# A decoder layer on one core: norm roots behind whole gate blocks, gate blocks in pairs that share a bank, and small products on zeros at the start

## The chip, the cores and the metric

The kernel runs on one core of a Trainium2 chip. Times are microseconds (us) of device time for one launch. A core has five engines that run beside each other and meet through semaphores: TensorE (PE in the profile, with its weight loads as PEld), VectorE (DVE), ScalarE (ACT), GpSimd (POOL) and SyncE (SP), which only issues transfers.

## The reference

One layer of a decoder in float32, for 1024 tokens of width 1024:

```python
f1 = swiglu(rms_norm(h, ffn1_pre_g[l]), ffn1_w_in[l], ffn1_w_out[l])   # silu(gate) * up, then @ w_out; D_FF = 2816
h = h + HALF_STEP * rms_norm(f1, ffn1_post_g[l])
u = rms_norm(h, mix_pre_g[l])
p_rwkv, p_swa, q_mem, gate_logits = _split(u @ w_in[l], IN_SIZES)
...                                                    # y_a: RWKV-7, y_b: sliding window, y_c: attention into memory
mem_n = rms_norm(mem, mem_norm_g[l])                   # memory: 256 tokens; keys and values are mem_n @ w_kv
...
merged = g_a * (y_a @ w_branch[l, 0]) + g_b * (y_b @ w_branch[l, 1]) + g_c * (y_c @ w_branch[l, 2])
h = h + rms_norm(merged @ w_out[l], mix_post_g[l])
f2 = swiglu(rms_norm(h, ffn2_pre_g[l]), ffn2_w_in[l], ffn2_w_out[l])
h = h + HALF_STEP * rms_norm(f2, ffn2_post_g[l])
```

`rms_norm` divides each token by the root of its mean square, so it needs a sum over all features before any product of the normalized value can start.

## The kernel before

**Products.** Activations lie with features on the partitions and tokens on the free axis, in two halves of 512 tokens (h0, h1). Every float32 operand is split into a high part (`w_hi`, `u`) and a low part (`w_lo`, the odd tile of a pair), and each product is three matmuls in `mm3`: high by high (L247), high by low (L248), low by high (L249). Weights come from DRAM in strips of 128 x 512 (`w_raw`, 256 KB, issued by SP, four buffers); ACT makes the high part (L154), VectorE the low part (L156), and eight pairs of such operands may be alive. A strip serves 12 matmuls.

**The FFNs** use a scheme of seven products in the place of eight (Strassen and Winograd): their input is turned into factors b11, t1, t2, b22, t3, b21, t4, which are sums of quarters of the normalized x. The gate's product of one block of 128 features needs only h0: a lower half (b11, strip `lower`, 12 matmuls) and an upper half (b21, strip `upper`, 12 matmuls). Such a *gate block* of 24 matmuls can run before h1 is normalized. The first `FIRST` blocks of each FFN run so: their lower part m1 and their gate g are parked in DRAM (`first_d`) and come back later for the *rest* of the block (60 matmuls). The other blocks run whole (*pair*, 84 matmuls).

**The first FFN's start.** The first `UNSCALED` gate blocks do not wait for the norm. `unscaled_gates` multiplies x by the gain only (`split`), takes the products, and multiplies m1 and g by the reciprocal root `rs` afterwards (`finish`: m1 on POOL, L429, g on VectorE, L430). Meanwhile ACT squares x (L313) and POOL adds the squares (L317), for h0 and for h1.

**A gate block before** takes two banks of PSUM: lower in `px`, upper in `py`. ACT copies `px` away (L459), and VectorE adds it to `py` (L465); ACT then applies Silu.

**A norm's root** (`rstd`): four small matmuls with ones sum the squares over the partitions (`ps_ms`, L275); VectorE takes the reciprocal root with 13 small operations on 128 x 4 numbers (L280 to L291: `rsm`, `rsh`, `rsy`, `rsq`); four matmuls with the identity spread it over the partitions (`ps_rs`, L297). `factors_norm` then scales x by gain and root (L358), `factors_first` and `factors_part` form and split the factors (L304 and others).

**Memory.** While VectorE inverts triangular blocks for RWKV (`rwkv_invert`: L881 and L882, in a chain of steps that shrink), TensorE runs the mixer's input products. Then `memory_kv` normalizes the memory tokens by a `rstd` of its own and makes keys (`pq`, 128 x 256, scaled into `km` by VectorE) and values. The mixer's 24 gate blocks (`gate_block`, `pgate`, 48 matmuls on two strips each) follow; the first `GATES_FIRST` of them come before the RWKV chain, whose first product is `gram` (L913).

**What sets the order.** The tile framework's scheduler orders each engine's instructions; `high_priority(offset)` moves an instruction ahead by so many places (`lead` is 300, `urgent` 1000). `plan` lists the weight strips in the order in which they are loaded. PSUM has four banks for large products and four for small ones.

Of the kernel before, what the change touches and what calls it, by code (L numbers as in the profile page):

```python
# [33 lines left out]
FIRST = {"ffn1": 13, "ffn2": 13}  # L34
UNSCALED = 8
# [13 lines left out]
GATES_FIRST = 8  # L49
ATT_ROW = {f: i for i, f in enumerate(ATT_BLOCKS)}  # L50
# [32 lines left out]
class Builder:  # L83
# [4 lines left out]
    def plan(self):  # L88
        seq = []
        for f in ("ffn1", "ffn2"):  # L90
            if f == "ffn1":
                items = [(f + "_" + q, j) for q in ("lower", "upper") for j in (0, 1)]
            else:
                items = [(f + "_gate", j) for j in (0, 1)]
            items += [(f + "_gate", j) for j in range(2, FIRST[f])] + [(f + "_rest", j) for j in range(FIRST[f])]
# [16 lines left out]
        for name, i in seq:  # L112
            f, _, kind = name.partition("_")
            halves = (slice(0, 4), slice(4, 8))
            if kind in ("gate", "rest", "pair"):
                for j in (i,) if kind == "gate" else (i, i + KF):
                    self.raws += [(self.io[f + "_in"][j][:, q], "in" if j >= KF else None) for q in halves]
# [188 lines left out]
    def sum_squares(self, xs, pool, engine=None):  # L306

        nc = self.nc
        n = xs[0].shape[1]
        acc = None  # L310
        for x in xs:
            sq = pool.tile([P, n], F32, tag=f"sq{n}", name="sq", bufs=3)
            nc.scalar.activation(sq, x, ACT.Square)  # L313
            if acc is None:
                acc = sq
            else:
                (engine or nc.vector).tensor_tensor(acc, acc, sq, ALU.add)  # L317
        return acc
# [32 lines left out]
    def factors_norm(self, xs, part, gname, pool, rs=None, engine=None):  # L351
# [3 lines left out]
        if rs is None:  # L355
            rs = self.rstd([self.sum_squares(xs, pool, engine)], D, pool, hi - lo)[:, : hi - lo]
# [14 lines left out]
    def factors_begin(self, pool):  # L371
# [3 lines left out]
        self.t2, self.t3 = ([pool.tile([P, TH], F32, tag="t", name="t", bufs=8) for _ in range(KH)] for _ in (0, 1))  # L375
# [35 lines left out]
    def unscaled_gates(self, f, x, pool, first_d):  # L411

        nc, V, G = self.nc, self.nc.vector, self.nc.gpsimd
        raw = [(self.u_tile(), self.u_tile()) for _ in range(KD)]

# [7 lines left out]
        def half(name, j, xs, last):  # L423
            ps = self.psum("py" if last else "px")
            self.product(ps, self.take(f + "_" + name, j), xs, True, True)
            return ps

        def finish(m1, g):
            G.tensor_tensor(m1, m1, rs, ALU.mult)  # L429
            V.tensor_tensor(g, g, rs, ALU.mult)  # L430
            nc.scalar.activation(g, g, ACT.Silu)
            return m1, g

        split(range(KH))
        m = [self.gate_product(half("lower", j, raw[:KH], False), pool) for j in (0, 1)]
        split(range(KH, KD))
        done = [(a, self.gate_sum(half("upper", j, raw[KH:], True), a, pool)) for j, a in enumerate(m)]
        sq = self.sum_squares([t[0] for t in x], pool, G)

        def gate(j):  # L440
            a = self.gate_product(half("gate", j, raw[:KH], False), pool)
            return a, self.gate_sum(half("gate", j, raw[KH:], True), a, pool)

        done.append(gate(2))
        ps = self.rstd([sq], D, pool)
        rs = self.u_tile(F32)
        nc.scalar.copy(rs, ps)
        for j in range(UNSCALED):
            if j >= len(done):
                done.append(gate(j))  # L450
            self.store_first(first_d, j, *finish(*done[j]))
            if j == 2:
                self.factors_norm(x, HALVES[0], f + "_pre_g", pool, rs)
                self.factors_first(x)

    def gate_product(self, px, pool):
        x = pool.tile([P, TH], F32, tag="px", name="m1", bufs=3)
        with self.tc.high_priority(offset=self.urgent):
            self.nc.scalar.copy(x, px)  # L459
        return x  # L460

    def gate_sum(self, py, x, pool):
        g = pool.tile([P, TH], F32, tag="gate", name="g", bufs=5)
        with self.tc.high_priority(offset=self.urgent):
            self.nc.vector.tensor_tensor(g, py, x, ALU.add)  # L465
        return g

    def store_first(self, first_d, j, m1, g):
        self.nc.gpsimd.dma_start(first_d[j, 0], m1)
        self.nc.gpsimd.dma_start(first_d[j, 1], g)  # L470

    def ffn_in(self, f, x, fact_d, first_d, parts, norm, pre=None):

        nc, V = self.nc, self.nc.vector
        with self.tc.tile_pool(reuse_waits="tile", name="ffn_in", bufs=2) as pool:
            self.stage, self.stage_pool = "in", pool
            if pre:
# [12 lines left out]
    def ffn_in_gate(self, name, j, pool):  # L490
# [538 lines left out]
    def memory_kv(self, pool, km_d, vm_d):  # L1029
# [497 lines left out]
```

## Time and profile before

| | us |
|---|---|
| median of 3 runs (2409.64 to 2413.92) | 2411.68 |
| the profiled execution | 2412.76 |
| its span | 2411.0 |
| TensorE busy | 2310.9 |
| VectorE busy | 1674.9 |
| ScalarE busy | 975.7 |
| GpSimd busy | 266.7 |

A row of a timeline reads: start, length, engine, line, operation, output<-inputs, shapes, number, and in brackets the idle time ahead with what ended it. In a table by windows, each engine's busy time in that stretch stands with its instructions in brackets; PEclk is the granted clock of TensorE, 1.00 at full speed. Matmuls overlap, so that their spacing, not their length, is their price.

### The profile page before, as it was taken

What the parts mean: (1) busy time and instruction counts of PE and PEld (TensorE: products, weight loads), DVE (VectorE), ACT (ScalarE), POOL (GpSimd) and SP (SyncE); (2) the same over time, 40 slices, a digit from 0 to 9 for tenths busy, and PEclk for the clock granted to TensorE, in tenths of its full rate; (3) what the DMA queues carried; (4) which work ended last, traced back from release to release, by engine and by line L of the source; (5) the groups of instructions that cost most, each with busy time, mean ns of one, the idle gap of its engine ahead of it and who ended that gap; (6) DMA issues with size and microseconds to landing.
All of it is one profiled execution on the core that took longest, in us unless ns stands there. A gap on an engine that the chain in (4) does not pass through costs nothing.

```text
span 2411.0 us, 34086 instructions
## 1 busy us (share of the span) xinstructions
PE 2310.9 (96%) x12176; PEld 1872.9 (78%) x12176; DVE 1674.9 (69%) x2719; ACT 975.7 (40%) x1833; POOL 266.7 (11%) x379
## 2 busy tenths in 40 slices
PE   7799999999999999799999999999999999999997
PEld 5588888787887778678776887778887788887887
DVE  7988765676787767981444447666898786667675
ACT  6422233444545343222335445524553223344551
POOL 5311110100000000200220000042011111100000
PEclk9899999999999999999999999999999999999998
DMA  5455532587632435334334534364465543338763
GB/s 202 165 171 184 169 105 97 180 274 234 226 130 92 151 107 210 102 133 147 115 119 144 165 110 147 109 209 154 153 205 181 199 166 118 109 123 289 239 217 107
DMA packets 218441, 389.38 MB, mean 162 GB/s; under 512 B 39296, under 2 KB 67456, under 8 KB 218016
## 3 DMA queue, kind: packets, MB, share of 16 engines
q1 hardware_dynamic: 185472, 305.08, 39.2%
q0 software_dynamic: 16480, 54.01, 6.0%
q10 hardware_dynamic: 16320, 28.12, 3.4%
q8 instruction: 96, 1.57, 0.3%
q14 instruction: 73, 0.60, 0.1%
HBM read 277.55 MB, written 108.53 MB: 160 GB/s over the span
## 4 chain that ended last, share of the span: by engine, by line
PE 73%; DVE 13%; DMA 5%; issue 4%; ACT 3%; POOL 1%; SPq 0%; DVEq 0%; ACTq 0%; POOLq 0%
PE px L247 5%; PE px L248 5%; PE px L249 5%; PE pgate L247 4%; PE pgate L249 3%; PE pgate L248 3%; PE po L247 3%; PE po L248 3%; PE po L249 3%; PE pz L247 3%; PE pz L248 3%; PE pz L249 3%; PE pu L247 2%; PE pu L248 2%; PE pu L249 2%
## 5 line engine op out<-in xcount | busy, mean ns | idle before, releaser
L154 ACT CAST w_hi<-w_raw 128x512 fp32r<-128x512 f32 x566 | 349.0, 620 | 786.0 <-PE px L248 138.7
L156 DVE TENSOR_TENSOR w_lo<-w_raw,w_hi 128x512 fp32r<-128x512 f32 x558 | 401.9, 723 | 224.1 <-ACT w_hi L154 218.9
L247 PE MATMUL px<-u,w_hi 128*128 128x512 f32 x352 | 140.1, 398 | 19.7 <-ACT w_hi L154 19.1
L247 PE MATMUL po<-u,w_hi 128*128 128x512 f32 (+1 forms) x396 | 147.9, 374 | 8.1 <-DVE g L552 4.3
L247 PE MATMUL pgate<-u,w_hi 128*128 128x512 f32 x384 | 154.3, 402 | 0.0
L249 PE MATMUL pgate<-u,w_lo 128*128 128x512 f32 x384 | 153.7, 400 | 0.0
L248 PE MATMUL pgate<-u,w_hi 128*128 128x512 f32 x384 | 153.0, 398 | 0.0
L248 PE MATMUL po<-u,w_hi 128*128 128x512 f32 (+1 forms) x396 | 147.1, 372 | 0.0
L249 PE MATMUL po<-u,w_lo 128*128 128x512 f32 (+1 forms) x396 | 147.0, 371 | 0.0
L247 PE MATMUL px<-f,w_hi 128*128 128x512 f32 x352 | 137.3, 390 | 3.4 <-DVE u L518 1.6
L247 PE MATMUL pz<-u,w_hi 128*128 128x512 f32 x352 | 137.8, 391 | 2.8 <-DVE m L518 2.8
L249 PE MATMUL px<-u,w_lo 128*128 128x512 f32 x352 | 139.6, 397 | 0.2 <-DVE w_lo L156 0.2
L248 PE MATMUL px<-u,w_hi 128*128 128x512 f32 x352 | 138.9, 395 | 0.0
L249 PE MATMUL pz<-u,w_lo 128*128 128x512 f32 x352 | 137.1, 389 | 0.0
L248 PE MATMUL pz<-u,w_hi 128*128 128x512 f32 x352 | 137.0, 389 | 0.0
L248 PE MATMUL px<-f,w_hi 128*128 128x512 f32 x352 | 137.0, 389 | 0.0
L249 PE MATMUL px<-f,w_lo 128*128 128x512 f32 x352 | 137.0, 389 | 0.0
L303 ACT CAST u<-hid 128x512 fp32r<-128x512 f32 x154 | 95.1, 620 | 92.7 <-DMA hid<-fact_d 91.7
L304 DVE TENSOR_TENSOR u<-hid,u 128x512 fp32r<-128x512 f32 x154 | 105.3, 687 | 32.2 <-ACT u L303 31.4
L537 POOL DMA_DIRECT2D fact_d<-g x88 | 47.5, 539 | 606.8 <-DVE g L536 281.5
L249 PE MATMUL pu<-u,w_lo 128*128 128x512 f32 x264 | 102.7, 389 | 0.0
L248 PE MATMUL pu<-u,w_hi 128*128 128x512 f32 x264 | 102.7, 389 | 0.0
(361 smaller groups left out, 5465.7 us busy)
## 6 DMA issues: line engine op xcount, KB each, us to landing
w_raw<-in_ffn_in SPq DMA_DIRECT2D x228, 256.0 KB
w_raw<-in_ffn_out SPq DMA_DIRECT2D x198, 256.0 KB
hid<-fact_d SPq DMA_DIRECT2D x154, 256.0 KB
w_raw<-in_win SPq DMA_DIRECT2D x112, 256.0 KB
fact_d<-g POOLq DMA_DIRECT2D x88, 256.0 KB, 2.8
fact_d<-h POOLq DMA_DIRECT2D x66, 256.0 KB, 3.4
gate_d<-gate SPq DMA_DIRECT2D x24, 512.0 KB
pk_d<-pk ACTq DMA_DIRECT2D x4, 2560.0 KB
```

Of the source, the lines that this page charges most:

```text
L154: self.nc.scalar.copy(hi, x)
L156: (engine or self.nc.vector).tensor_tensor(lo, x, hi.bitcast(F32), ALU.subtract)
L247: mm(out, wh, xh, start=first, stop=False, **kw)
L248: mm(out, wh, xl, start=False, stop=False, **kw)
L249: mm(out, wl, xh, start=False, stop=last, **kw)
L303: self.nc.scalar.copy(hi, x)
L304: self.nc.vector.tensor_tensor(lo, x, hi.bitcast(F32), ALU.subtract)
L537: store = lambda n, t: nc.gpsimd.dma_start(fact_d[FACTORS.index(n), j // 2], t)
```

## The change

- *Pairs in one bank each* (`gate_pair`): two blocks j and j+1 run in the order lower j, lower j+1, upper j, upper j+1. The upper half accumulates on top of the lower half in the same bank. ACT copies the lower part out in between (the upper product must wait for that copy), and takes the Silu straight from the bank. VectorE's addition of L465 goes for the blocks that run ahead; whole blocks keep it.
- `FIRST` goes from 13 to 16 in the first FFN and from 13 to 14 in the second; `UNSCALED` from 8 to 6. Of the six, blocks 0 to 3 are scaled afterwards by VectorE, m1 and g; blocks 4 and 5 are scaled by VectorE as it takes them out of the bank (`scale`).
- POOL's sums of squares and its scalings of m1 move to VectorE.
- `rstd(between=...)`: a gate pair is emitted between the sum over the partitions and the spreading of the root, and these small matmuls keep their place in program order. In the first FFN pair (2, 3) stands there for h0 and pair (8, 9) for h1; in memory, four mixer gate blocks (`GATES_MEM`), whose strips `plan` lists ahead of memory's. `memory_norm`, the part of `memory_kv` ahead of the root, is emitted before `rwkv_invert`.
- At the start, fourteen 128 x 128 matmuls of zeros (`warm`) and one small ACT operation run while the first loads are under way; the first weight strip is issued ahead of most of x, and x is loaded from two queues.
- t3 and t2 swap the order in which their tiles are taken.

```diff
-FIRST = {"ffn1": 13, "ffn2": 13}
-UNSCALED = 8
+FIRST = {"ffn1": 16, "ffn2": 14}
+UNSCALED = 6
+WARM = 14
+GATES_MEM = 4
...
-                (engine or nc.vector).tensor_tensor(acc, acc, sq, ALU.add)
+                nc.vector.tensor_tensor(acc, acc, sq, ALU.add)
...
-        self.t2, self.t3 = ([pool.tile([P, TH], F32, tag="t", name="t", bufs=8) for _ in range(KH)] for _ in (0, 1))
+        self.t3, self.t2 = ([pool.tile([P, TH], F32, tag="t", name="t", bufs=8) for _ in range(KH)] for _ in (0, 1))
...
+        def scale(t, ps):
+            with self.tc.high_priority(offset=self.urgent):
+                V.tensor_tensor(t, ps, rs, ALU.mult)
+
+        m_tile = lambda: pool.tile([P, TH], F32, tag="t", name="m1", bufs=8)
+        self.prefetch()
+        split(range(KH))
+        done = []
+        done += self.gate_pair(f, 0, lower, upper, pool, m_tile, between=lambda: split(range(KH, KD)))
+        sq = self.sum_squares([t[0] for t in x], pool)
+        ps = self.rstd([sq], D, pool, between=lambda: done.extend(self.gate_pair(f, 2, lower, upper, pool, m_tile)))
+        rs = self.u_tile(F32)
+        with self.tc.high_priority(offset=self.lead):
+            nc.scalar.copy(rs, ps)
+        for j, (m, g) in enumerate(done):
+            V.tensor_tensor(m, m, rs, ALU.mult)
             V.tensor_tensor(g, g, rs, ALU.mult)
...
+        self.factors_norm(x, HALVES[0], f + "_pre_g", pool, rs)
+        self.factors_first(x)
+        for j in range(4, UNSCALED, 2):
+            for i, (m, g) in enumerate(self.gate_pair(f, j, lower, upper, pool, m_tile, scale)):
+                self.store_first(first_d, j + i, m, g, g)
+
+    def gate_pair(self, f, j, lower, upper, pool, m_tile, evict=None, between=None, silu=False):
+
+        def copy(t, ps, func=ACT.Copy):
+            with self.tc.high_priority(offset=self.urgent):
+                self.nc.scalar.activation(t, ps, func)
+
+        pss, ms, gs = [], [], []
+        for i in (0, 1):
+            ps = self.psum("px")
+            self.product(ps, self.take(f + "_lower", j + i), lower, True)
+            pss.append(ps)
+            ms.append(m_tile())
+            (evict or copy)(ms[-1], ps)
+        if between:
+            between()
+        for i, ps in enumerate(pss):
+            self.product(ps, self.take(f + "_upper", j + i), upper, last=True)
+            gs.append(pool.tile([P, TH], F32, tag="gate", name="g", bufs=5))
+            copy(gs[-1], ps, ACT.Silu) if silu else (evict or copy)(gs[-1], ps)
+        return list(zip(ms, gs))
...
-                self.memory_kv(mp, km_d, vm_d)
-            for g in range(GATES_FIRST):
+                self.memory_kv(mp, km_d, vm_d, lambda: [self.gate_block(g, u, gp, gate_d) for g in range(GATES_MEM)])
+            for g in range(GATES_MEM, GATES_FIRST):
                 self.gate_block(g, u, gp, gate_d)
...
+    def warm(self, x):
+        ...
+        with self.tc.high_priority(offset=self.urgent):
+            nc.vector.memset(x, 0.0)
+            nc.scalar.activation(x[:, :1], x[:, :1], ACT.Square)
+            ps = self.psum("ps_ms")
+            for _ in range(WARM):
+                nc.tensor.matmul(ps[:, :P], x[:, P : 2 * P], x[:, 2 * P : 3 * P], start=True, stop=True)
```

How the instructions stand now. First TensorE at the end of the unscaled blocks of the first FFN. Before, this was the place of the root's spreading, in the upper half of block 3 (numbers tell tiles apart; `u_126` to `u_129` are unnormalized x):

```order
L247 MATMUL py_460<-u_126,w_hi_201 128x512
L248 MATMUL py_460<-u_127,w_hi_201 128x512
L249 MATMUL py_460<-u_126,w_lo_203 128x512
L247 MATMUL py_460<-u_128,w_hi_201 128x512
L297 MATMUL ps_rs_377<-ident_68,rsy_361 128x128 x4
L248 MATMUL py_460<-u_129,w_hi_201 128x512
L249 MATMUL py_460<-u_128,w_lo_203 128x512
```

Now `ps_rs` stands 45 rows ahead of the following, which is the end of block 5 (`px_520`) and the start of pair (6, 7), the first with normalized operands `u_467` (high) and `u_468` (low):

```order
L247 MATMUL px_520<-u_144,w_hi_353 128x512
L248 MATMUL px_520<-u_145,w_hi_353 128x512
L249 MATMUL px_520<-u_144,w_lo_355 128x512
L247 MATMUL px_587<-u_467,w_hi_374 128x512
L247 MATMUL px_608<-u_467,w_hi_394 128x512
L247 MATMUL px_750<-u_467,w_hi_523 128x512
L247 MATMUL px_771<-u_467,w_hi_543 128x512
L248 MATMUL px_587<-u_468,w_hi_374 128x512
L249 MATMUL px_587<-u_467,w_lo_376 128x512
```

TensorE takes the four products of one high operand for four blocks first, and then needs its low part. VectorE at the same place: before, the evictions `g` (L465) stand between the norms (L358) and the low parts of the factors (L304), and the first low part, `u_408`, follows eight norms:

```order
L358 SCALAR_TENSOR_TENSOR acc_93<-acc_93,vecs_64,u_382 128x512
L358 SCALAR_TENSOR_TENSOR acc_97<-acc_97,vecs_64,u_382 128x512
L156 TENSOR_TENSOR w_lo_559<-w_raw_487,w_hi_557 128x512
L358 SCALAR_TENSOR_TENSOR acc_94<-acc_94,vecs_64,u_382 128x512
L358 SCALAR_TENSOR_TENSOR acc_98<-acc_98,vecs_64,u_382 128x512
L465 TENSOR_TENSOR g_573<-py_554,m1_552 128x512
L156 TENSOR_TENSOR w_lo_585<-w_raw_508,w_hi_583 128x512
L304 TENSOR_TENSOR u_408<-acc_91,u_407 128x512
```

After, the last scaled eviction, `g_579` out of the bank of block 5, stands ahead of six of the norms and of `u_468`:

```order
L358 SCALAR_TENSOR_TENSOR acc_91<-acc_91,vecs_64,u_437 128x512
L358 SCALAR_TENSOR_TENSOR acc_95<-acc_95,vecs_64,u_437 128x512
L426 TENSOR_TENSOR g_579<-px_520,u_437 128x512
L156 TENSOR_TENSOR w_lo_592<-w_raw_521,w_hi_590 128x512
L358 SCALAR_TENSOR_TENSOR acc_92<-acc_92,vecs_64,u_437 128x512
L358 SCALAR_TENSOR_TENSOR acc_96<-acc_96,vecs_64,u_437 128x512
L358 SCALAR_TENSOR_TENSOR acc_93<-acc_93,vecs_64,u_437 128x512
L358 SCALAR_TENSOR_TENSOR acc_97<-acc_97,vecs_64,u_437 128x512
L358 SCALAR_TENSOR_TENSOR acc_94<-acc_94,vecs_64,u_437 128x512
L358 SCALAR_TENSOR_TENSOR acc_98<-acc_98,vecs_64,u_437 128x512
L304 TENSOR_TENSOR u_468<-acc_91,u_467 128x512
```

So `u_468` cannot be made before block 5 is out of its bank. The second place is TensorE at memory's root. Before, only the keys' products (`pq`, 128x256) stand between the sum and the spreading, and the values' products follow:

```order
L247 MATMUL pq_8904<-mem_hi_8719,w_hi_8780 128x256
L248 MATMUL pq_8904<-mem_lo_8720,w_hi_8780 128x256
L249 MATMUL pq_8904<-mem_hi_8719,w_lo_8782 128x256
L297 MATMUL ps_rs_8767<-ident_68,rsy_8751 128x128 x2
L247 MATMUL pq_8932<-w_hi_8814,mem_hi_8719 128x512
L248 MATMUL pq_8932<-w_lo_8816,mem_hi_8719 128x512
```

After, four mixer gate blocks (`pgate`, 192 matmuls) stand there, and the keys' products follow the spreading:

```order
L247 MATMUL pgate_8985<-u_6035,w_hi_8796 128x512
L248 MATMUL pgate_8985<-u_6036,w_hi_8796 128x512
L249 MATMUL pgate_8985<-u_6035,w_lo_8798 128x512
L297 MATMUL ps_rs_9050<-ident_68,rsy_8770 128x128 x2
L247 MATMUL pq_9067<-mem_hi_7988,w_hi_8856 128x256
L248 MATMUL pq_9067<-mem_lo_7989,w_hi_8856 128x256
```

More of the change, by code (lines that the diff above doesn't have):

```diff
@@ L90, in plan @@
         for f in ("ffn1", "ffn2"):
[L91 to L95, printed above, removed]
+            items = [(f + "_" + q, j + i) for j in range(0, FIRST[f], 2) for q in ("lower", "upper") for i in (0, 1)]
+            items += [(f + "_rest", j) for j in range(FIRST[f])]
             items += [(f + "_pair", j) for j in range(FIRST[f], KF)]
@@ L114, in plan @@
             halves = (slice(0, 4), slice(4, 8))
-            if kind in ("gate", "rest", "pair"):
-                for j in (i,) if kind == "gate" else (i, i + KF):
+            if kind in ("rest", "pair"):
+                for j in (i, i + KF):
                     self.raws += [(self.io[f + "_in"][j][:, q], "in" if j >= KF else None) for q in halves]
@@ L348, in project_first, with factors_norm @@
             self.nc.scalar.copy(raw[:, 8 + h * TH : 8 + (h + 1) * TH], o)
-    def factors_norm(self, xs, part, gname, pool, rs=None, engine=None):
+    def factors_norm(self, xs, part, gname, pool, rs=None, between=None):
         h, lo, hi = part
@@ L411, in unscaled_gates @@
     def unscaled_gates(self, f, x, pool, first_d):
-        nc, V, G = self.nc, self.nc.vector, self.nc.gpsimd
+        nc, V = self.nc, self.nc.vector
         raw = [(self.u_tile(), self.u_tile()) for _ in range(KD)]
+        lower, upper = raw[:KH], raw[KH:]
         def split(ks):
@@ L421, in split @@
                 V.scalar_tensor_tensor(lo, x[k][0], g, hi.bitcast(F32), ALU.mult, ALU.subtract)
[L423 to L429, printed above, removed]
-            V.tensor_tensor(g, g, rs, ALU.mult)
-            nc.scalar.activation(g, g, ACT.Silu)
-            return m1, g
-        split(range(KH))
@@ L435, in unscaled_gates @@
[L435 to L460, printed above, removed]
@@ L470, in store_first, with gates_ahead @@
+    def store_first(self, first_d, j, m, g, x=None):
+        if x is not None:
+            self.nc.scalar.activation(g, x, ACT.Silu)
+        self.nc.gpsimd.dma_start(first_d[j, 0], m)
         self.nc.gpsimd.dma_start(first_d[j, 1], g)
+    def gates_ahead(self, f, j, pool, first_d):
+        px = lambda: pool.tile([P, TH], F32, tag="px", name="m1", bufs=3)
+        for i, (m, g) in enumerate(self.gate_pair(f, j, self.fs["b11"], self.fs["b21"], pool, px, silu=True)):
+            self.store_first(first_d, j + i, m, g)
@@ L476, in ffn_in @@
             self.stage, self.stage_pool = "in", pool
+            ahead = iter(range(UNSCALED if pre else 0, FIRST[f], 2))
+            between = lambda: self.gates_ahead(f, next(ahead), pool, first_d)
             if pre:
                 pre(pool)
+                between()
             self.factors_begin(pool)
             for part in parts:
-                norm(part, pool)
+                norm(part, pool, between)
                 self.factors_part(x, part, pool)
             self.factors_end(x)
-            for j in range(UNSCALED if pre else 0, FIRST[f]):
-                self.store_first(first_d, j, *self.ffn_in_gate(f + "_gate", j, pool)[1:])
+            for j in ahead:
+                self.gates_ahead(f, j, pool, first_d)
             for j in range(KF):
@@ L493, in ffn_in_gate @@
         self.product(px, self.take(name, j), fs["b11"], True)
-        x = self.gate_product(px, pool)
+        x = pool.tile([P, TH], F32, tag="px", name="m1", bufs=3)
+        with self.tc.high_priority(offset=self.urgent):
+            nc.scalar.copy(x, px)
         self.product(py, self.take(name, j), fs["b21"], True, True)
-        g = self.gate_sum(py, x, pool)
+        g = pool.tile([P, TH], F32, tag="gate", name="g", bufs=5)
+        with self.tc.high_priority(offset=self.urgent):
+            nc.vector.tensor_tensor(g, py, x, ALU.add)
         nc.scalar.activation(g, g, ACT.Silu)
@@ L1438, in build, with ready @@
                     self.factors_first(x)
-                def ready(part, pool):
+                def ready(part, pool, between):
                     post(part, [t[:, part[1] : part[2]] for t in xr], pool)
```

49 lines of the change are left out of this document (27 added, 22 removed).

## The prediction

> **What bounds the kernel now.** I read the page first, then TensorE's waits, then the timeline of TensorE at the waits, then a table by windows, and last VectorE's rows in the same stretches.
>
> ```profile
> span 2411.0 us, 34086 instructions
> PE 2310.9 (96%) x12176; PEld 1872.9 (78%) x12176; DVE 1674.9 (69%) x2719; ACT 975.7 (40%) x1833; POOL 266.7 (11%) x379
> ```
>
> TensorE is busy for 96% of the span, and the change leaves its real products as many as they were. So it can win two things only: the 100.1 us in which TensorE stands (2411.0 − 2310.9), and the time in which its clock is low after standing. The profiled execution took 2412.76 us, 1.8 us beside its span, and lies 1.1 us above the median of 2411.68; I sum against 2412.8 and take the 1.1 us off at the end.
>
> Whom TensorE waited for (total us, times, longest):
>
> ```profile
> PE ps_rs L297 <- DVE rsy L291: 30.3, 8, 15.6
> PE px L247 <- ACT w_hi L154: 19.4, 3, 10.8
> PE pq L247 <- DVE km L1055: 1.4, 1, 1.4
> ```
>
> The first two rows are half of all standing, and the change rewrites the code around them. Where they lie (start, length, and in brackets the idle time ahead):
>
> ```profile
> 8.35 0.79 PE L247 MATMUL px<-u,w_hi 128*128 128x512 f32 x1 [8.35 <-ACT w_hi L154]
> ...
> 33.20 0.39 PE L249 MATMUL py<-u,w_lo 128*128 128x512 f32 x1
> ...
> 34.11 0.39 PE L247 MATMUL py<-u,w_hi 128*128 128x512 f32 x1
> 40.88 1.86 PE L297 MATMUL ps_rs<-ident,rsy 128*128 128x128 f32 x7 [6.39 <-DVE rsy L291]
> ...
> 78.37 1.86 PE L297 MATMUL ps_rs<-ident,rsy 128*128 128x128 f32 x7 [6.19 <-DVE rsy L291]
> ...
> 115.47 0.80 PE L247 MATMUL px<-u,w_hi 128*128 128x512 f32 x1 [10.79 <-ACT w_hi L154]
> ...
> 1027.42 1.20 PE L297 MATMUL ps_rs<-ident,rsy 128*128 128x128 f32 x4 [15.61 <-DVE rsy L291]
> ```
>
> Four matmuls from 33.20 to 34.11 give the spacing at full clock, 0.2275 us. A gate block is 24 matmuls, 5.46 us. By windows:
>
> ```profile
> core 0: us, PE busy (x) PEld busy (x) DVE busy (x) ACT busy (x) POOL busy (x), PEclk, DMA share, GB/s
> 8.35:33.00 24.65, 24.32 (x97) 19.21 (x98) 17.64 (x19) 17.97 (x32) 15.19 (x11) 1.00 0.67 229
> ...
> 43.50:68.00 24.50, 23.98 (x106) 19.40 (x106) 24.39 (x29) 14.60 (x26) 18.91 (x16) 0.97 0.44 151
> ...
> 100.00:122.00 22.00, 11.21 (x39) 8.37 (x38) 20.72 (x35) 11.81 (x22) 1.62 (x3) 0.77 0.54 180
> 122.00:250.00 128.00, 127.53 (x561) 104.48 (x560) 107.10 (x171) 35.99 (x59) 16.18 (x30) 1.00 0.55 183
> 1000.00:1030.00 30.00, 13.02 (x105) 12.55 (x105) 29.86 (x38) 5.97 (x11) 9.15 (x5) 0.74 0.32 106
> 1030.00:1060.00 30.00, 30.00 (x121) 24.42 (x122) 27.93 (x34) 10.09 (x16) 0.00 (x0) 0.92 0.42 141
> ```
>
> Three things are to be seen. In 43.5 to 68 and in 1000 to 1030 VectorE has no idle time (24.39 of 24.50, 29.86 of 30.00): it is what the low places wait for. The clock column falls where TensorE stood. From 122 on TensorE hardly stands (127.53 of 128). The gain is therefore to be looked for ahead of 122 us, near 1010 us, and in the second FFN's copy of the same stage.
>
> **Why VectorE is late there**, by groups over 0 to 117 us (two of VectorE, two of POOL) and by its timeline with ACT's:
>
> ```profile
> L156 DVE TENSOR_TENSOR w_lo<-w_raw,w_hi 128x512 fp32r<-128x512 f32 x27 | 27.1, 1018 | 6.4 <-ACT w_hi L154 6.4
> L465 DVE TENSOR_TENSOR g<-py,m 128x512 f32<-128x512 f32 x13 | 8.8, 681 | 2.4 <-PE py L249 2.1 <-issue 0.3
> ...
> L317 POOL TENSOR_TENSOR sq<-sq 128x512 f32<-128x512 f32 x14 | 20.4, 1460 | 16.0 <-ACT sq L313 15.5
> L429 POOL TENSOR_TENSOR m<-m,u 128x512 f32<-128x512 f32 x8 | 16.5, 2066 | 10.4 <-ACT u L447 5.8 <-DVE g L465 4.5
> ```
> ```profile
> 27.91 0.63 ACT L313 ACTIVATE sq<-acc 128x512 f32<-128x512 f32 x1 [1.40 <-POOL sq L317]
> ```
> ```profile
> 29.08 1.36 DVE L156 TENSOR_TENSOR w_lo<-w_raw,w_hi 128x512 fp32r<-128x512 f32 x1 [4.13 <-ACT w_hi L154]
> ...
> 34.96 0.15 DVE L280 TENSOR_SCALAR rsm<-ps_ms 128x4 f32<-128x4 f32 x1
> ...
> 38.37 0.69 DVE L156 TENSOR_TENSOR w_lo<-w_raw,w_hi 128x512 fp32r<-128x512 f32 x1
> 38.98 0.15 DVE L291 SCALAR_TENSOR_TENSOR rsy<-rsq,rsy 128x4 f32<-128x4 f32 x1
> ...
> 40.67 0.16 DVE L291 SCALAR_TENSOR_TENSOR rsy<-rsq,rsy 128x4 f32<-128x4 f32 x1
> ```
>
> One strip's low part costs 0.69 us (38.37), or 0.61 as spacing (38.37 to 38.98). Beside POOL's adds it took 1.36 at 29.08, and its mean is 1018 ns. POOL also holds ACT up (1.40 us ahead of the square at 27.91); the weight cast queued behind that square then keeps VectorE waiting 4.13 us. So POOL's 22 operations are dearer than their own row.
>
> **Part 1, the start.** The first product waits 8.35 us for its weight. I take 7.5 with the strip loaded first (ends: 6.5, no change). Its twelve matmuls need 2.73 us at the full spacing; in fact ACT could copy them out only here:
>
> ```profile
> 14.16 0.59 ACT L459 COPY m<-px 128x512 f32<-128x512 f32 x1 [0.52 <-PE px L249]
> ```
>
> So they took about 5.6 us, 2.9 lost to a low clock and late operands. Fourteen small matmuls at 0.47 us (1.86 for the four at 40.88, which leave seven records) run 6.5 us ahead of them, in time in which TensorE stands anyway. I take 1.0 of the 2.9 back (ends 0 and 2.9), since the splits of x on ACT also pace this product. [...]
>
> **Part 2, the first norm of FFN 1.** The new order has 36 matmuls (8.2 us) between the sum and the broadcast, for 22 (5.0) before. VectorE has 26 full operations ahead of the root and 11 among its 13 small ones. From about 6 us on, 26 × 0.60 plus 3 us of waits for loads (7.0 of standing in the window from 8.35, less the 4.13 behind ACT) is 24.6; the chain adds 11 × 0.60, 13 × 0.15 and 1.1 for one slow shift, so the root is there near 34.3. The 14 adds for 1.46 us on POOL now cost 14 × 0.60 = 8.4 on VectorE, which this counts; in return the spacing of w_lo returns to 0.60. TensorE stands at the broadcast after 7.5 + 1.9 + 97 × 0.2275 = 31.5. A wait of 2.8 stays of 6.39, plus 1.9 for the broadcast (1.86) and 1.2 of low clock (0 to 2.1; the window after 43.5 has clock 0.97, 0.7 us, and as much again lies before it).
>
> **A new wait.** Only six blocks go unscaled now, not eight. After blocks 4 and 5 TensorE is at 34.3 + 1.9 + 10.7 + 1.2 = 48.1 and needs normalized, split factors. On VectorE stand 16 operations (9.6 us) from 37.2 to the last eviction of block 5, which cannot start before 48.1, then that one, a strip's low part, six norms and the first factor's low part: 9 × 0.60 = 5.4 gives 53.6. Four matmuls (0.9) need the high part only. So about 4.7 us of standing and 1.4 of clock, nothing of which was there before. Ends: 0, and 10 if VectorE is 5 us later.
>
> **The second norm.** TensorE then needs 44 matmuls (10.0) and 1.4 of clock to end blocks 6 and 7 and reaches the second broadcast after ten blocks, at 53.6 + 10.0 + 1.4 + 10.9 = 76.0, with two whole blocks (10.9 us) of cover for a chain of 5.7 (34.96 to 40.67), so the 6.19 us go. At full clock the broadcast takes 1.2. Then six blocks, 32.8 us, stand ahead of the first rest block. What VectorE must do meanwhile can be read off this trace:
>
> ```profile
> 80.48 1.41 DVE L358 SCALAR_TENSOR_TENSOR acc<-acc,vecs,ps_rs 128x512 f32<-128x512 f32 x2 [1.53 <-PE ps_rs L297]
> ...
> 114.08 0.68 DVE L181 TENSOR_TENSOR w_raw<-w_sum,w_raw 128x512 f32<-128x512 f32 x1
> ```
>
> Before, 51 operations stand from the one to the other (33.6 us), and TensorE starts 1.4 later. Now it is 49, with no add of L465 among them: 1.2 + 29.4 + 1.4 = 32 against 1.2 + 32.8 = 34, from the broadcast on. The 10.79 us go, with 2 us to spare.
>
> **Sum of FFN 1.** Before, 13 blocks are 71.0 us of 115.47, 44.5 over; after 115.47 there are 18 matmuls (39 less 4.7 / 0.2275) in 6.5 us, 2.3 lost to the clock: 46.8. After: 7.5 + 1.9 + 2.8 + 1.9 + 1.2 + 4.7 + 1.4 + 1.2 = 22.6, so the first rest starts near 87.4 + 22.6 = 110.0, with 16 blocks done. Gain 24.2 (ends 10 and 36).
>
> **Part 3, memory.** VectorE's chain there:
>
> ```profile
> 1008.34 0.15 DVE L280 TENSOR_SCALAR rsm<-ps_ms 128x2 f32<-128x2 f32 x1
> ...
> 1017.34 2.25 DVE L881 TENSOR_TENSOR itmp<-inv 128x986 f32<-128x986 f32 x1
> ...
> 1027.12 0.15 DVE L291 SCALAR_TENSOR_TENSOR rsy<-rsq,rsy 128x2 f32<-128x2 f32 x1
> ```
>
> The small steps take 18.9 us, since each stands behind a step of the inverse (up to 2.25). Four gate blocks of the mixer are moved between sum and broadcast: 4 × 48 × 0.2275 = 43.7 us of cover. That takes away 15.61, the 1.37 behind it, 0.08 × 30 = 2.4 of low clock from 1030 on and about 0.6 inside the broadcast: 20.0 (ends 17 and 21). The gates' eight low parts (4.8 us) now fall on VectorE beside the inverse, whose end and first reader are these:
>
> ```profile
> 1080.35 0.28 DVE L882 TENSOR_TENSOR inv<-inv,itmp 128x62 f32<-128x62 f32 x1
> ```
> ```profile
> 1130.68 1.16 PE L913 MATMUL gram<-f 64*128 64x128 f32 x16
> ```
>
> The reader comes 20 us sooner and the end some 5 later; 25 of 50 us are left. The moved blocks' loads stand on SP's queue ahead of those for memory: eight strips of 256 KB in 43.7 us, at a DMA share of 0.32.
>
> **Part 4, FFN 2.** Its 13 adds (13 × 0.60 = 7.8 us of VectorE) go, and there is one more block of cover. From 1751 to 2000 TensorE waited:
>
> ```profile
> PE pz L247 <- DVE m L518: 2.6, 3, 1.0
> PE px L247 <- DVE u L518: 1.6, 2, 0.8
> PE px L247 <- DVE up L531: 1.5, 1, 1.5
> ```
>
> That is 5.7; these are readers of banks, not of weights, so I take 2.5 (ends −1 and 5.7, the loss being a wait at the norms, whose cover falls from 14 and 12 matmuls to 11). More first blocks also mean three more parked pairs in FFN 1, under a DMA share of 0.55 and TensorE 127.53 of 128: nothing.
>
> **Sum:** 24.2 + 20.0 + 2.5 = 46.7. 2412.8 − 46.7 = 2366.1, less 1.1: 2365 us.
>
> **Rivals.** *Full gain:* no new wait, no wait at the first broadcast: 4.7 + 1.4 + 2.8 + 1.2 more, 2355. For it: w_lo back at 0.60 may put VectorE ahead. Against: six norms stand behind that eviction. 0.13. *VectorE stays the bound of FFN 1:* up to the first rest block it gets 14 adds, 8 scalings, 4 scaled evictions and 6 more low parts for 8 scalings and 13 adds, 11 operations or 6.6 us more; if POOL's adds were not what slowed it, nothing pays for these, the new wait comes to 10, the spare 2 us are used up and 8 more: FFN 1 gives about 10, the sum is 32 and the time 2379. For it speaks 24.39 of 24.50; against it the 1018 ns. 0.20. *Slower:* upper and lower half share one bank, so an upper product may start only when ACT has copied the lower half away. The other lower product covers 2.73 us, and a copy takes 0.59. If the copy came 3.7 us late in each of the 30 blocks, 1.5 us a block would eat all 46.7, about 2413; beyond that it is slower. Against: ACT works 14.60 of 24.50 us in the busiest such window, and these copies go ahead of its other work. 0.03. *Nothing happens,* because the scheduler lets VectorE's roots fall back by as much as TensorE's cover grows: within 0.2%, which is about what a measurement tells from no change: 0.02. The forecast, between 2357 and 2374, has 0.62.
>
> **Range.** 2352 to 2385: it takes in full gain and most of the second rival. Faster 0.95, same 0.02, slower 0.03.
>
> **What the new profile would show.** Row ps_rs of the waits down from 30.3 to about 11, none near 1010; the row px for w_hi down to about 7.5; a wait of 4 to 5 us near 49 at px for u of L304; first rest near 110. Wrong would make it: upper products that wait for ACT's copy, VectorE still full at the second norm, or a wait at the reader of the inverse near 1110.

## The result, and the profile after

The changed kernel takes 2372.9 us (median of 4 runs, 2369.66 to 2376.14) against 2411.19 (2409.64 to 2413.92): a ratio of 0.984 (95% interval 0.9823 to 0.9857), 38.3 us faster. Forecast were 2365 and 46.7; 2372.9 is near the upper end of the 2357 to 2374 named there. The profiled execution took 2373.79 us.

```profile
span 2372.1 us, 34157 instructions
PE 2308.0 (97%) x12204; PEld 1874.0 (79%) x12204; DVE 1657.1 (70%) x2720; ACT 971.1 (41%) x1828; POOL 234.4 (10%) x365
```

TensorE stands 64.1 us, for 100.1 (its busy time now includes the products on zeros, a row of 4.87 us). Its waits now:

```profile
PE px L248 <- DVE u L304: 4.2, 1, 4.2
PE pq L247 <- DVE km L1074: 3.9, 2, 3.2
...
PE px L247 <- ACT u L421: 2.6, 1, 2.6
PE px L247 <- DVE up L546: 2.3, 1, 2.3
PE px L247 <- ACT w_hi L154: 2.3, 1, 2.3
...
PE ps_rs L297 <- DVE rsy L291: 1.8, 3, 1.4
```

The spreading of the roots (`ps_rs`) falls from 30.3 to 1.8 us; five waits of 2 to 4 us stand in its place. Where the time came from is read off the same products in both kernels: of each row (min/median/max of its duration) the first and the last start count. `pz` starts with the first rest block and ends with FFN 2's input stage; `po` starts FFN 1's output stage; `gram` is the first reader of the inverse; `pb` follows the mixer. Before, then after:

```profile
L247 PE MATMUL pz<-u,w_hi x352: 387/389/504, 120.6 to 2171.7; 128*128 128x512 f32 x176
...
L247 PE MATMUL po<-u,w_hi x396: 278/389/797, 467.6 to 2393.3; 128*128 128x512 f32 x154, 128*128 128x256 f32 x44
...
L913 PE MATMUL gram<-f x256: 272/272/374, 1130.7 to 1276.5; 64*128 64x128 f32 x128
...
L247 PE MATMUL pb<-u,w_hi x128: 387/389/628, 1470.9 to 1602.3; 128*128 128x512 f32 x128
```
```profile
L247 PE MATMUL pz<-u,w_hi x352: 387/389/496, 112.0 to 2134.4; 128*128 128x512 f32 x176
...
L247 PE MATMUL po<-u,w_hi x396: 278/389/792, 450.9 to 2353.8; 128*128 128x512 f32 x154, 128*128 128x256 f32 x44
...
L928 PE MATMUL gram<-f x256: 272/272/373, 1100.5 to 1246.3; 64*128 64x128 f32 x128
...
L247 PE MATMUL pb<-u,w_hi x128: 388/389/628, 1440.8 to 1572.9; 128*128 128x512 f32 x128
```

The lead is 8.6 us at the first `pz` (with three more blocks done, 16.4 us of work, so 25.0), 16.7 at the first `po`, 30.2 at `gram`, 30.1 at `pb`, 37.3 at the last `pz`, 38.9 at the end of the span. So FFN 1's input stage gave 16.7 (forecast 24.2), memory 13.5 (20.0), FFN 2's input stage 7.2 (2.5).

TensorE's timeline at the places of the prediction:

```profile
9.03 0.73 PE L247 MATMUL px<-u,w_hi 128*128 128x512 f32 x2 [2.64 <-ACT u L421]
...
32.92 1.13 PE L297 MATMUL ps_rs<-ident,rsy 128*128 128x128 f32 x8
...
45.77 1.19 PE L247 MATMUL px<-u,w_hi 128*128 128x512 f32 x4 [1.02 <-ACT u L303]
51.18 0.79 PE L248 MATMUL px<-u,w_hi 128*128 128x512 f32 x1 [4.22 <-DVE u L304]
...
75.29 1.05 PE L297 MATMUL ps_rs<-ident,rsy 128*128 128x128 f32 x8
...
108.86 0.39 PE L247 MATMUL px<-u,w_hi 128*128 128x512 f32 x1
...
150.42 0.47 PE L247 MATMUL px<-f,w_hi 128*128 128x512 f32 x1 [2.29 <-DVE up L546]
...
209.67 0.77 PE L247 MATMUL px<-f,w_hi 128*128 128x512 f32 x1 [2.28 <-ACT w_hi L154]
...
1027.04 0.60 PE L297 MATMUL ps_rs<-ident,rsy 128*128 128x128 f32 x4
...
1039.72 0.47 PE L247 MATMUL pq<-w_hi,mem_hi 128*128 128x512 f32 x1 [0.68 <-DVE km L1074]
1043.83 0.79 PE L247 MATMUL pq<-w_hi,mem_hi 128*128 128x512 f32 x1 [3.17 <-DVE km L1074]
```

All three spreadings now start without a bracket, that is, without a wait. The new wait near 49 us is there (5.24 us in two rows; 4.7 were forecast). The first rest block starts at 108.86 (110.0 were forecast). Not forecast are the waits near 148, 207 and 1040. By windows, with the clock behind each wait (the column after POOL's busy time):

```profile
43.50:68.00 24.50, 19.26 (x78) 15.08 (x77) 16.45 (x37) 11.57 (x21) 3.78 (x7) 0.86 0.54 188
...
122.00:250.00 128.00, 122.98 (x526) 100.29 (x525) 100.52 (x159) 33.03 (x54) 16.20 (x30) 0.97 0.53 177
147.00:158.00 11.00, 8.71 (x31) 6.72 (x31) 8.69 (x14) 2.80 (x5) 0.59 (x2) 0.84 0.33 122
206.00:217.00 11.00, 8.72 (x33) 6.74 (x32) 8.42 (x14) 2.63 (x5) 0.54 (x1) 0.84 0.20 72
...
1039.00:1050.00 11.00, 7.15 (x20) 5.36 (x20) 10.93 (x15) 3.52 (x6) 4.95 (x3) 0.69 0.54 180
...
1875.00:2000.00 125.00, 124.88 (x551) 102.80 (x550) 100.06 (x159) 36.01 (x59) 17.81 (x33) 1.00 0.50 171
```

Between 122 and 250 TensorE was busy for 127.53 of 128 before and is for 122.98 now, and the clock column costs more: 0.16 × 11 = 1.8 us at each of two places. The rows agree: the twelve products from 150.42 and from 209.67 take 4.41 and 4.32 us, for 2.73 at full spacing, so 1.7 and 1.6 more. FFN 2's rest blocks went the other way, to 124.88 of 125 from this row of the kernel before:

```profile
1875.00:2000.00 125.00, 120.03 (x525) 97.58 (x524) 101.28 (x161) 33.79 (x55) 17.80 (x33) 1.00 0.52 176
```

VectorE at the two new places:

```profile
148.25 0.69 DVE L179 TENSOR_TENSOR w_sum<-w_raw 128x512 f32<-128x512 f32 x1 [3.35 <-DMA w_raw<-in_ffn_in]
148.98 0.69 DVE L180 TENSOR_TENSOR w_raw<-w_raw 128x512 f32<-128x512 f32 x1
149.59 0.68 DVE L546 TENSOR_TENSOR up<-px,m 128x512 f32<-128x512 f32 x1
...
1038.41 0.83 DVE L897 TENSOR_TENSOR inv<-inv,itmp 128x650 f32<-128x650 f32 x1
1039.16 0.42 DVE L1074 TENSOR_TENSOR km<-pq,mem_rs 128x256 f32<-128x256 f32 x1
...
1041.63 1.81 DVE L896 TENSOR_TENSOR itmp<-inv 128x572 f32<-128x572 f32 x1
1043.37 0.41 DVE L1074 TENSOR_TENSOR km<-pq,mem_rs 128x256 f32<-128x256 f32 x1
```

Near 148, the eviction `up`, for which TensorE waits, stands behind a sum of the next block's strips, and that sum waits for a transfer. Near 1040, the scalings that free the keys' banks stand behind steps of the inverse.

### The profile page after: what moved, and what is told of

The parts are those of the page before. It is cut to its first block, busy times and chain, and to the rows that moved or that the text cites. A ratio compares the mean times of both kernels' runs of the same rounds, so it can differ in the third digit from the quotient of the medians.

```text
span 2372.1 us, 34157 instructions
## 1 busy us (share of the span) xinstructions
PE 2308.0 (97%) x12204; PEld 1874.0 (79%) x12204; DVE 1657.1 (70%) x2720; ACT 971.1 (41%) x1828; POOL 234.4 (10%) x365
## 4 chain that ended last, share of the span: by engine, by line
PE 75%; DVE 12%; DMA 6%; issue 3%; ACT 3%; SPq 0%; DVEq 0%; ACTq 0%
PE px L248 7%; PE px L249 7%; PE px L247 7%; PE pgate L247 3%; PE pgate L249 3%; PE pz L247 3%; PE pz L248 3%; PE pz L249 3%; PE pgate L248 3%; PE po L247 2%; PE po L248 2%; PE po L249 2%; PE pu L248 2%; PE pu L247 2%; PE pu L249 2%
## 5 line engine op out<-in xcount | busy, mean ns | idle before, releaser
L156 DVE TENSOR_TENSOR w_lo<-w_raw,w_hi 128x512 fp32r<-128x512 f32 x558 | 394.4, 709 | 209.2 <-ACT w_hi L154 203.0
L248 PE MATMUL px<-u,w_hi 128*128 128x512 f32 x376 | 147.7, 394 | 4.3 <-DVE u L304 4.2
L247 PE MATMUL px<-u,w_hi 128*128 128x512 f32 x376 | 146.6, 392 | 3.7 <-ACT u L421 2.6
L249 PE MATMUL px<-u,w_lo 128*128 128x512 f32 x376 | 147.1, 392 | 0.2 <-DVE w_lo L156 0.2
L304 DVE TENSOR_TENSOR u<-hid,u 128x512 fp32r<-128x512 f32 x154 | 105.2, 686 | 31.4 <-ACT u L303 30.6
```

The costliest lines, as they stand in the source:

```text
L156: (engine or self.nc.vector).tensor_tensor(lo, x, hi.bitcast(F32), ALU.subtract)
L247: mm(out, wh, xh, start=first, stop=False, **kw)
L248: mm(out, wh, xl, start=False, stop=False, **kw)
L249: mm(out, wl, xh, start=False, stop=last, **kw)
L304: self.nc.vector.tensor_tensor(lo, x, hi.bitcast(F32), ALU.subtract)
```

## The experiments

Each edit is made on the changed kernel. The runs were made in three groups beside the kernel before (medians 2410.58, 2410.80 and 2407.49), and the single edits' ratios have intervals of about ±0.2% (5 us), as wide as some of the differences; so where a verdict is about one wait, the wait's row decides and the ratio only agrees or not.

| edit | median us | ratio to before (95% interval) |
|---|---|---|
| none (the changed kernel) | 2372.9 | 0.984 (0.9823 to 0.9857) |
| keys copied out by ACT | 2367.11 | 0.982 (0.9796 to 0.9843) |
| eight unscaled blocks | 2363.31 | 0.9793 (0.9774 to 0.9813) |
| parked parts on POOL's queue | 2366.14 | 0.981 (0.9786 to 0.9834) |
| memory part undone | 2384.32 | 0.9882 (0.9862 to 0.9901) |
| parked parts and hidden factors on POOL's queue | 2362.66 | 0.9807 (0.9786 to 0.9827) |
| no products on zeros | 2370.75 | 0.9837 (0.9821 to 0.9854) |
| POOL adds the squares | 2383.13 | 0.9884 (0.9865 to 0.9903) |
| FFN 2: two banks and an addition | 2371.69 | 0.9841 (0.9826 to 0.9856) |
| FFN 2: 12 blocks ahead | 2368.85 | 0.9833 (0.9808 to 0.9857) |
| FFN 1: 14 blocks ahead | 2375.04 | 0.9862 (0.9839 to 0.9885) |
| two stores left out | 2366.13 | 0.9825 (0.9799 to 0.9851) |
| the four that helped, together | 2351.68 | 0.9764 (0.9741 to 0.9787) |

**Keys copied out by ACT.** ACT frees the banks at once; VectorE scales the copies in its own time.

```diff
-            V.tensor_tensor(t, ps[:, :MEM], rs, ALU.mult)
-            nc.scalar.dma_start(km_d[:, h], t)
+            with self.tc.high_priority(offset=self.urgent):
+                nc.scalar.copy(t, ps[:, :MEM])          # four km tiles in place of two
+            V.tensor_tensor(t, t, rs, ALU.mult)         # stores of km: after those of the values
```

> The changed kernel, but the keys' four products are copied out of their banks by ACT at once, and VectorE scales the copies later; the stores of the keys follow those of the values. Theory A (the values' products wait because VectorE's scaling stands behind the inverse): the waits of pq for km (3.9 us) go, and with them the low clock behind them (6.8 us at half speed, 3.4 us): about 2366 against 2373. Theory B (POOL's low parts for the memory weights are late by then and only hide behind that wait): pq waits for w_lo in its place, and the time stays at 2372 to 2374.

2367.11. The row "pq <- km" is gone; three waits for VectorE's low parts stand there (0.57, 0.92 and 0.87 us), without the low clock:

```profile
1034.00:1050.00 16.00, 13.50 (x58) 9.90 (x57) 15.79 (x25) 4.88 (x9) 3.31 (x2) 1.00 0.38 131
```

The wait came from the order on VectorE, as theory A has it. Theory B was right in kind: a shorter wait for weights had hidden behind this one, though VectorE's low parts, not POOL's, are late.

**Eight unscaled blocks.**

```diff
-UNSCALED = 6
+UNSCALED = 8
...
                 pre(pool)
-                between()
```

> The changed kernel with eight unscaled blocks for six, the pair ahead of the second sum left out, so that ten blocks stand ahead of the second spreading as before. Theory A (the 5.2 us at 44.7 to 51.2 us are a wait for the factors that two more blocks of cover take away): no wait there, no low clock behind it (6.8 us at half speed, 3.4 us): 2364 to 2366. Theory B (VectorE bounds this stage, and four more scaled evictions, 2.4 us, bring it back later): the wait comes again at the first rest block, and the time is 2370 to 2374.

2363.31, just below theory A's figure. The whole stretch of the new wait is full:

```profile
33.00:80.00 47.00, 47.00 (x219) 39.21 (x218) 42.46 (x79) 26.67 (x47) 12.72 (x24) 1.00 0.68 227
80.00:110.00 30.00, 29.73 (x131) 23.98 (x129) 29.14 (x49) 18.89 (x36) 4.73 (x9) 1.00 0.61 204
```

Only 0.27 us come back later, so VectorE did not hold TensorE up, though it is nearly full there (29.14 of 30). The first `pz` comes at 103.5, for 112.0 in the changed kernel; 1.4 of these 8.5 us are a first product that came earlier (7.62 for 9.03). The step from eight to six unscaled blocks was a costly part of this change.

**Parked parts on POOL's queue, and then the first hidden factors too.**

```diff
-            nc.sync.dma_start(m1, first_d[j, 0])
-            nc.sync.dma_start(g0, first_d[j, 1])
+            nc.gpsimd.dma_start(m1, first_d[j, 0])
+            nc.gpsimd.dma_start(g0, first_d[j, 1])
...                                                     # second kernel only, in out_hidden:
-                self.nc.sync.dma_start(x, fact_d[FACTORS.index(OUT_FACTOR[ph]), i])
+                e = self.nc.gpsimd if ph == "a11" and i < 3 else self.nc.sync
+                e.dma_start(x, fact_d[FACTORS.index(OUT_FACTOR[ph]), i])
```

> The changed kernel, but the parked m1 and g come back over POOL's queue in place of SP's (both FFNs). Theory A (SP's queue: the load of m1 waits for its buffer, and the next block's strips stand behind it): the waits at 148 and 207 us (2.3 each, with 3.4 us of low clock in all) go: about 2365. Theory B (the strips land late because the stores of the finished factors, 256 KB each, run at the same time): the waits stay, 2372 to 2375.

> The kernel with the parked m1 and g on POOL's queue, and the first three loads of the hidden factors (which wait on SP for a store to end, 4 us near 133) on POOL's queue too. Moving m1 and g alone took away the wait near 207 but left the one near 148. Theory A (whatever waits at the head of SP's queue delays the strips behind it): the wait near 148 goes as well, about 2363. Theory B (the strips only land late because of traffic beside them): it stays at about 2.3 us, 2365 to 2368.

2366.14 and 2362.66. The wait near 207 is gone in both. But it is absent too in four kernels that leave this stretch as it was (memory part undone, no products on zeros, POOL's adds, 12 blocks in FFN 2), and lies near 264 in another, so its absence proves nothing. The wait near 148 stays in both; in the second kernel, where nothing but strips is left on SP's queue:

```profile
155.92 0.76 PE L247 MATMUL px<-f,w_hi 128*128 128x512 f32 x1 [2.28 <-DVE up L546]
```

So theory A of both runs, that loads at the head of SP's queue delay the strips, falls for this wait. The times alone would have seemed to confirm it. Both are below 2372.9, but their intervals overlap that of the changed kernel, and no run here shows what they gained from.

**Two stores left out.** After the second rest block, t2 and t4 are not stored, and their readers take the next pair's factors; this changes what is computed.

```diff
-            store("t2", t2)
+            if (f, j) != ("ffn1", 1):
+                store("t2", t2)
...                                                     # t4 likewise
```

> The changed kernel without two of the five stores (t2 and t4, 256 KB each) that follow the second rest block of FFN 1; their readers take the next pair's factors instead, so the output differs. This is for the wait of 1.8 to 2.7 us near 148 that all kernels with the new first stage show and that no change of queue moved. Theory A (the strips land late because these stores run beside them, 2 MB in all from 141 to 149): with 1.5 MB the strips land some 1.5 us sooner and the wait falls to about 0.8. Theory B (the strips are issued late, when VectorE frees their buffers, and the stores don't matter): the wait stays within 0.4 us of 2.3. The time itself, 2370 to 2374, tells little.

```profile
151.17 0.47 PE L247 MATMUL px<-f,w_hi 128*128 128x512 f32 x1 [1.25 <-DVE up L546]
```

1.25 us, where the same place showed 1.84 to 2.68 in the profiles of all eleven other kernels with 16 blocks ahead. This lies between the two theories. VectorE waits 2.61 us there for the strip, for 3.35, and the strip is added up 5.1 us after it is issued, for 5.9. That transfers beside the strips are part of the cause is what this one profile suggests, no more. What is left of the wait was not taken apart: SP's queue spends much of this stretch waiting for VectorE to free the strips' buffers (27.4 us of 108 to 153 in the changed kernel), and that part was not tried.

**Memory part undone.** `GATES_MEM` is 0 and `rstd` gets no `between`; the memory squares stay early.

> The changed kernel without the memory part: no gate blocks between sum and spreading, memory's strips ahead of all gates again; memory's squares still early. By the landmarks of the two traces this part is worth 13.3 us, so 2386. If it is worth what the prediction gave it (20.0), 2393. If the gates only move a wait that returns at the chain of RWKV, below 2380.

```profile
1006.26 1.19 PE L297 MATMUL ps_rs<-ident,rsy 128*128 128x128 f32 x4 [16.54 <-DVE rsy L291]
```

The wait is back (15.61 before), and 11.4 us with it, in line with the 13.5 of the landmarks and not with 20.

**No products on zeros.** `warm` keeps its memset and the ACT operation.

> The changed kernel without the fourteen products on zeros (the early ACT operation stays). Theory A (they bring the clock up): the first twelve real products run at half speed again, 5.6 us in place of 3.0, and with waits for operands partly absorbed, 2374.5 to 2376. Theory B (the split of x on ACT paces these products anyway, the clock is irrelevant): 2372 to 2374. [...]

2370.75, with an interval that takes in the changed kernel's ratio: no cost that the time shows, as the second theory has it; its reason, ACT's splits, was not tested by itself. In its profile the first products run slow:

```profile
8.68 0.63 PE L248 MATMUL px<-u,w_hi 128*128 128x512 f32 x1
```

The next two start 0.43 and 0.42 us apart, for 0.23 in the changed kernel from 10.15 on; the clock column reads 1.00 there all the same, so that only the spacing tells. The first product comes 1.37 us sooner (7.66 for 9.03), and the wait for the factors ends 0.94 us later (52.12 for 51.18). So at most 2.3 us of what the clock gave reach that point, and the time shows none of it. Nor do the products on zeros always bring the clock up: in five of the twelve profiles with them (keys by ACT, memory part undone, both moves to POOL's queue, 12 blocks in FFN 2, two stores left out) real products near 11 us still start 0.42 or 0.43 us apart.

Without the products on zeros, the real ones are slow for 6.2 us in this trace (7.66 to 13.88). In the kernel before, which has no products on zeros either, the first twelve take 5.57 us (8.35 to 13.92), and from 14.35 on they start 0.23 apart.

**POOL adds the squares.**

```diff
-                nc.vector.tensor_tensor(acc, acc, sq, ALU.add)
+                (engine or nc.vector).tensor_tensor(acc, acc, sq, ALU.add)   # engine: POOL for FFN 1's two sums
```

> The changed kernel with the fourteen adds of squares on POOL again. Theory A (POOL's adds slow VectorE and hold up ACT): the root of the first half comes later than TensorE, a wait of 4 to 8 us at the first spreading comes back with low clock, 2379 to 2384. Theory B (the adds cost VectorE 8.4 us that it now has free): the factors come sooner and the wait at 45 to 51 shrinks, 2366 to 2370.

2383.13, 10 us slower. Groups of the first 60 us, of VectorE and of POOL:

```profile
L156 DVE TENSOR_TENSOR w_lo<-w_raw,w_hi 128x512 fp32r<-128x512 f32 x20 | 15.6, 803 | 3.3 <-ACT w_hi L154 3.3
L422 DVE SCALAR_TENSOR_TENSOR u<-acc,vecs,u 128x512 fp32r<-128x512 f32 x8 | 9.1, 1153 | 1.1 <-ACT u L421 1.1
```
```profile
L317 POOL TENSOR_TENSOR sq<-sq 128x512 f32<-128x512 f32 x14 | 20.7, 1480 | 19.9 <-ACT sq L313 19.5
```

The size is theory A's, the place is not: TensorE waits 2.82 and 1.51 us for the scaled evictions and 4.02 for the factors, not at the spreading. The same two groups in the changed kernel:

```profile
L156 DVE TENSOR_TENSOR w_lo<-w_raw,w_hi 128x512 fp32r<-128x512 f32 x22 | 14.9, 685 | 6.8 <-ACT w_hi L154 6.8
...
L422 DVE SCALAR_TENSOR_TENSOR u<-acc,vecs,u 128x512 fp32r<-128x512 f32 x8 | 6.0, 746 | 0.3 <-ACT u L421 0.3
```

VectorE's low parts take 803 ns for 685, the splits 1153 for 746. Fourteen adds on POOL cost more than the fourteen on VectorE that they save.

**FFN 1 with 14 blocks ahead.**

> The changed kernel with 14 blocks ahead in FFN 1 in place of 16, so that four blocks (21.8 us) stand between the second spreading and the first rest block in place of six (32.8). Theory A (VectorE needs 32 us there, so cover decides): a wait of about 10 us for w_hi comes back near 98 us, with 1.7 to 3.4 us of low clock, 2380 to 2385. Theory B (VectorE is ahead by now, and more blocks only bring more parked parts): 2370 to 2374.

```profile
106.07 0.80 PE L247 MATMUL px<-u,w_hi 128*128 128x512 f32 x1 [8.52 <-ACT w_hi L154]
```

The wait comes as theory A has it (8.52 for 10), but the time, 2375.04, is not that far up. At the first `pz` the changed kernel is 9.6 us ahead (112.0 for 110.7, with two more blocks, 10.9 us, done), at the first `po` 3.3 (450.9 for 454.2). In between, this kernel has no wait near 148 or 207 at all, only 1.3 us in three small ones up to 300. So two more blocks of cover win the 8.52 us and pay much of it back in the rest blocks.

Why its rest blocks run free of these waits was not tried. The kernel before and this one have the same loads and the same five stores at the second rest block, and `up` stands behind the same sums, yet VectorE waits less for the strip than the changed kernel's 3.35 us. Before, then here:

```profile
153.13 0.69 DVE L179 TENSOR_TENSOR w_sum<-w_raw 128x512 f32<-128x512 f32 x1 [0.98 <-DMA w_raw<-in_ffn_in]
```
```profile
143.47 0.69 DVE L179 TENSOR_TENSOR w_sum<-w_raw 128x512 f32<-128x512 f32 x1 [0.97 <-DMA w_raw<-in_ffn_in]
```

So neither these transfers nor that order is enough to make TensorE wait. Both kernels stand for long just ahead of their rest blocks (10.79 and 8.52 us), which may give the loads and VectorE a lead; the runs do not tell this from the number of parked blocks.

**FFN 2, two banks and an addition; and 12 blocks ahead.**

> The changed kernel, but the fourteen gate blocks ahead of FFN 2 use two banks and VectorE's addition again, in the same order of pairs. By the landmarks FFN 2's first stage gained 7.3 us. Theory A (VectorE's 14 additions, 8.4 us, were what the rest blocks' waits came from): 5 to 7 us come back, 2378 to 2380. Theory B (the additional block of cover did it): 0 to 2 come back, 2373 to 2375.

> The changed kernel with 12 blocks ahead in FFN 2 in place of 14. Before, with 13 blocks, TensorE waited 5.7 us among the rest blocks there, and giving VectorE its 14 additions back did not bring those waits again. Theory A (the cover of the blocks ahead decides): with 10.9 us less of it the waits come back in full, 4 to 8 us, 2377 to 2381. Theory B (the order in pairs did it, which lets every operand be made in time): 2371 to 2375.

2371.69 and 2368.85. From 1700 to 2000 their waits sum to 1.7 and 1.1 us, so neither the 14 additions nor the cover alone brings the 5.7 us back. Either one may suffice, or the order in pairs is the cause; a kernel that undoes both was not run, and this stays open.

**The four together:** eight unscaled blocks, keys copied by ACT, both moves to POOL's queue.

> The four edits that each helped, together on the changed kernel: eight unscaled blocks, keys copied out by ACT, parked parts and the first hidden factors on POOL's queue. If the gains are of different stretches they add: 9.6 for the blocks, 5.8 for the keys, 6.8 to 10 for the queue, from 2372.9 to 2347 to 2351. [...]

2351.68 (2349.3 to 2355.27), ratio 0.9764 (0.9741 to 0.9787): some 20 us better than the changed kernel, with the intervals apart. The time lies just above the 2347 to 2351 of gains that add, and the runs reach from inside that range to 4 us above it, so it is not shown whether they add in full. What the moves to POOL's queue add to the other two edits was not measured apart.

## Why the prediction was right, and where it was off

- *The three waits for roots.* Right: 6.39, 6.19 and 15.61 us are gone. At the first spreading I kept 2.8 and the low clock; there was none: the slow shift that I priced 1.1 us extra took 0.17 without POOL beside it, and the root was there at 32.8, not 34.3. Wait, broadcast and clock came to 1.1 us for 5.9. With POOL's adds back, that operation took 0.90.
- *The new wait* near 49 was forecast at 4.7 us plus 1.4 of clock and came at 5.24. The clock column gives 0.14 × 24.5 = 3.4 (read in steps of 1 us, it is at 0.50 for 6.8 us, from 49.0 to 55.8), but a part of the low clock falls into the standing itself: the eleven products from 51.18 to 55.95 lose 2.3 (4.77 us for 2.50). The kernel with eight unscaled blocks shows its mechanism.
- *The start.* Off: 1.85 us credited; the first product came 0.7 later than before (9.03 for 8.35). In the twelve profiles of kernels with the products on zeros it comes between 7.54 and 9.40, so this figure was in part chance. The products on zeros are worth nothing that the times show.
- *The 10.79 us ahead of the first rest block.* Right: it started at 108.86, and 14 blocks for 16 bring 8.52 of them back. Up to here the sum held, 25.0 for 24.2, in part by luck: the first norm was 4.8 us cheaper than forecast, the start and the new wait dearer.
- *The step that failed* is the sentence that more first blocks cost nothing in the rest blocks, for which I read a mean DMA share of 0.55. Waits of 2.29, 0.45 and 2.28 us and 1.7 and 1.6 of clock are 8.3 us (before, these waits were 0.5), about what FFN 1 fell short from there on (25.0 less 16.7). With 14 blocks ahead these waits are not there. The cause is not settled: transfers beside the strips may be part of it, and so may the stand that went ahead of the rest blocks. What a mean over 128 us cannot show is VectorE's wait of 3.35 us for one strip.
- *Memory* was mis-sized by one row: I let the 1.37 us of `pq` for `km` go with the rest, without asking what stands ahead of `km` on VectorE. It grew to 3.85, and the low clock behind it cost 2.6 more: the twelve products from 1043.83 to 1049.12 take 5.29 us for 2.73 (the column's 0.31 × 11 = 3.4, at 0.50 for 6.8 us from 1042.3 to 1049.1, includes a part of the standing). 20.0 less 6.4 is 13.6; the landmarks say 13.5.
- *FFN 2* gave 7.2, not 2.5: I held its waits to be readers of banks that a lighter VectorE would not help, and they all but went; which part of the change took them away is open. That was luck, and it made up for a part of the rest: FFN 1 and memory fell 14.0 us short, and this is 4.7 over.
- *The rivals.* That the upper product waits for ACT's copy of the lower one: no such row appears in the waits. VectorE as the bound: not so (16.45 of 24.50 in 43.5 to 68; 47.00 of 47.00 for TensorE with eight unscaled blocks).
- *The signs.* No wait near 1010 and none at the reader of the inverse, as forecast. The figure of about 11 for the row of `ps_rs` does not follow from the prediction's own terms, which leave 30.3 − 3.6 − 6.2 − 15.6 = 4.9; 1.8 was measured. The row of `px` for `w_hi` was to keep 7.5 us of the start; the first product now waits for `u` (2.64), and the 2.28 of that row are the wait near 207.

## What to carry to other kernels

When a long wait goes, read what stands ahead of the next consumer in each engine's order: here two evictions that free banks, `km` and `up`, stood behind work that TensorE did not wait for yet. Cover is not free just because the stage behind it has room on average: here two more blocks gave 9.6 us, of which 3.3 were left at the next stage. Look at the few microseconds in which one strip must land, not at the mean. A change of many parts is worth undoing part by part even when it wins: one part (six unscaled blocks for eight) cost 10 us of its gain.

## What the runs showed of the hardware

A short wait has a low clock behind it in some profiled executions and none in others. Behind 2.29 us of standing near 148 the changed kernel's clock was 0.84 over 11 us; behind 2.54 us at the same place in the kernel with the four edits, and 2.48 in that with POOL's queue, it was 1.00:

```profile
139.50:150.50 11.00, 8.46 (x38) 6.73 (x37) 8.52 (x14) 2.91 (x5) 0.54 (x1) 1.00 0.52 179
```
```profile
149.00:160.00 11.00, 8.52 (x38) 6.75 (x37) 8.85 (x14) 2.91 (x5) 0.74 (x2) 1.00 0.50 175
```

So 2.29 us of standing had a low clock behind it, while 2.48 and 2.54 had none; what decides it was not shown. The difference may be one reason why runs of one kernel spread over 6 us and more: of the second kernel on POOL's queue, one run took 2370.61 us at a mean clock of 0.989 and another 2359.73 at 0.993. Which waits differed between them is not known.
